# Half of the modulation blocks computed on ScalarE and GpSimd instead of TensorE, in a two-layer diffusion backbone on one core

## The chip, the cores and the metric

The kernel runs on one core of one Trainium2 chip. A core has five engines, each with its own queue that it works off in order: PE (TensorE: matmuls, and transposes done as matmuls), DVE (VectorE), ACT (ScalarE), POOL (GpSimd) and SP, which here only issues DMAs. PE writes to PSUM (banks of 128 rows x 512 f32), everything else lies in SBUF. The metric is device time in microseconds (us), the median of three runs. A change of under 0.2% (some 3 us) can't be told from none.

## What is computed

Two layers over 256 latent and 256 context tokens of width 1024. A conditioning vector per sample (`c`) and one for the context (`c_ctx`) give, by a product with `w_mod`, six vectors of 1024 per layer: shift, scale and gate of the token mixer, and of the feed-forward part.

```python
for l in range(2):
    mod  = silu(c)     @ w_mod[l] + b_mod[l]     # 6 x 1024, for the latent tokens
    modc = silu(c_ctx) @ w_mod[l] + b_mod[l]     # 6 x 1024, for the context tokens
    sh1, sc1, gt1, sh2, sc2, gt2 = split(mod, 6)
    h  = rms_norm(xl, g_pre_mix[l]) * (1 + sc1) + sh1
    y  = token_mixer(h, ...)      # conv, attention and pooling branch, gated, projected
    xl = xl + gt1 * rms_norm(y, g_post_mix[l])
    h  = rms_norm(xl, g_pre_ffn[l]) * (1 + sc2) + sh2
    xl = xl + gt2 * rms_norm(swiglu(h, ...), g_post_ffn[l])
    # context tokens: the same with modc, in layer 0 only
```

The conv branch is a gated product, a depthwise convolution of 31 taps over 512 channels, a layer norm, SiLU and a projection. The attention branch has 8 heads of differential attention; each head's output is normalised (sub-norm).

## The kernel before

Activations lie with channels on the 128 partitions and tokens along the free axis: 512 tokens in layer 0, and in layer 1, where the context is needed for keys and values alone, 256 for most products. Each f32 operand is split into two f32r parts, hi and lo; a product is three matmuls (`mm3`, lines 331 to 333: hi·hi, hi·lo, lo·hi). Weights come in 302 units of 128x1024 f32, in the order of `weight_order`. For each unit SP loads `raw`, ACT writes `hi` (L347), DVE writes `lo = raw - hi` (L348); there are four buffers of each, so a unit is made ready some four units ahead of its matmuls.

A modulation block (`mod_block`) is 256 of the 6144 columns of `w_mod`, for both vectors: 24 blocks a layer, numbered `4*j + part`, where j is 0 to 5 for sh1, sc1, gt1, sh2, sc2, gt2. `mod_product` does eight f32 matmuls (L380; the trace has two records for each) of 32 columns, four of which stand side by side in the array. `mod_close` then brings the sums into place: for shifts and scales ACT copies them out, PE transposes them twice (L422), DVE reduces them into `modv`; for the gates (j of 2 and 5) ACT and DVE split them, PE spreads them over 128 rows by two matmuls a vector (L400, L401), DVE adds the bias and multiplies with the norm's gain into `G`. Blocks stand between other PE work: at the start, within the heads, within the last gating round (`new_modv_fill`), in the feed-forward, and under the end of each output projection.

Layer 0 runs: heads; the conv branch's gated product (`glu`); four pooling groups (`pool_group`: POOL sums of 256 to 271 columns); sub-norm; then three gating rounds of eight steps, `merge(1, ..)`, `merge(2, ..)`, `merge(0, ..)`, each step two units (24 matmuls of 512 columns for the gate, 24 or 12 for the branch). After each step of the first round ten convolution taps are queued on DVE (`S_B`), after each of the second twenty (`S_C`), until all 120 (L832) are out; then `norm`: POOL sums the four accumulators (L839, L842), PE takes the mean (L845), DVE subtracts it (L852), squares, a second matmul (L862), and so to `ya`, which `merge(0, ..)` reads. Then the output projection and the feed-forward follow. The queues' orders are fixed when the program is built, by a scheduler that plays the program through with its own costs.

Of the kernel before, what the change touches and what calls it, by code (L numbers as in the profile page):

```python
# [48 lines left out]
UW = 1024  # L50

# [144 lines left out]
def lay_mod(w):  # L196

    m = w["w_mod"].reshape(DEPTH, 2, 4, P, 24, 256)
    return np.ascontiguousarray(m.transpose(0, 4, 1, 3, 2, 5)).reshape(
        DEPTH * 48, P, UW)  # L200


class Net:
    def __init__(self, ctx, tc, io):
# [15 lines left out]
    BUFS = {"raw": 4, "hi": 4, "lo": 4, "rawx": 4, "hix": 2, "lox": 3, "mod": 2, "H": 4, "V": 18, "O": 8, "Q": 10,  # L220
            "E": 7, "A": 6, "T": 4, "S": 2, "G": 4, "row": 2, "rows": 3, "sq": 4, "K2": 2, "QD": 1, "QH": 2, "QL": 2, "tp": 2, "st": 25, "sh": 1,
# [130 lines left out]
    def mod_load(self, l, b, tag=None):  # L352

        raws = []
        src = self.io["wmod"]
        for kh in range(2):
            if tag is None or len(tag[0]) > 1:
                raw = self.t("mod" if tag is None else tag.popleft(), [P, UW])
                self.nc.sync.dma_start(out=raw, in_=src[l * 48 + b * 2 + kh])
# [27 lines left out]
    def mod_close(self, l, b, ps, gate=None):  # L387
# [155 lines left out]
    def out_proj(self, l, kind, nkp, acts, ntt, x, jg, tail, last, fill=()):  # L543
# [32 lines left out]
        for hf, kp in seq[:-last]:  # L576
            work(hf, kp, self.unit(kind, l, hf, kp), range(ntt))
            self.step(1)
        us = [(hf, kp, self.unit(kind, l, hf, kp)) for hf, kp in seq[-last:]]
# [168 lines left out]
    def subln(self, os, sg, n):  # L748

        nc = self.nc  # L750
        nh = len(os)
        ssq = self.ps(self.SUB_BK)
# [12 lines left out]
        for h in range(nh):  # L765
            bc = self.ps(self.BC_BK)
            rp = slice(32 * h, 32 * h + 32)
            pick = self.ident_r[rp, h:h + 1].to_broadcast([32, P])
            nc.tensor.matmul(bc[:, :n], pick, rh[rp, :n], start=True, stop=False)
            nc.tensor.matmul(bc[:, :n], pick, rl[rp, :n], start=False, stop=True)  # L770
# [7 lines left out]
    def glu(self, l, acts, n, after_first):  # L778
# [3 lines left out]
        for i in range(NCC):  # L782
# [9 lines left out]
            if i == 0 and after_first is not None:  # L792
                after_first()
# [3 lines left out]
    def conv_tasks(self, l, us, nseq, out):  # L797
# [20 lines left out]
        def tap(i, d):  # L818
            def f():
# [5 lines left out]
                if i in by_pool:  # L825
                    t = self.c2("tp")[:, 0:b - a]
# [104 lines left out]
    def layer(self, l, H, acts, first, xin, xnext, tail):  # L931
# [12 lines left out]
        if not need_ctx:  # L944
            us = self.glu(l, acts, n, None)
# [7 lines left out]
        self.new_G(l, 2)  # L953
        fill = deque(range(8, 12))
# [20 lines left out]
        if need_ctx:  # L975
            us = self.glu(l, acts, n, None)
# [45 lines left out]
        for n_ in range(KC):  # L1022
            merge(1, n_, yb, ("ao", l, n_), 0)
            self.step(self.S_B)
# [15 lines left out]
        for n_ in range(KC):  # L1040
            merge(2, n_, yc, ("po", l, n_ // 2) if n_ % 2 == 0 else None,
                  (n_ % 2) * 4)
            self.step(self.S_C)
        self.drain()
        x = self.load_x(xin, ntt, "Q")
        self.new_modv_fill(l)
        for n_ in range(KC):
            merge(0, n_, ya, ("co", l, n_ // 2) if n_ % 2 == 0 else None,
                  (n_ % 2) * 4)
            if self.fill:  # L1050
                self.fill.popleft()()
            if n_ >= 4 and self.fill:
                self.fill.popleft()()
        while self.fill:
            self.fill.popleft()()
# [23 lines left out]
        if need_ctx:  # L1079
            self.new_G(l, 5)  # L1080
        fill = todo
# [24 lines left out]
        for i in range(i0, NFF):  # L1106
# [5 lines left out]
            if fill:  # L1112
                self.mod_block(*fill.popleft(), bank=self.FF_BK)
        while fill:
# [3 lines left out]
        if need_ctx:  # L1118
            ahead = [((l + 1, 12), None), ((l + 1, 16), "OOOO"), ((l + 1, 13), "OOOO")]
        self.out_proj(l, "fo", NFF // 2, fa, ntt, x, 5, tail, self.LASTF[l],  # L1120
                      ahead)

    def new_modv_fill(self, l):

        self.fill = deque()
        for part in range(4):
            for j in (3, 4):
                if l > 0 and (part, j) in ((0, 3), (0, 4), (1, 3)):
                    continue
                self.fill.append(lambda b=j * 4 + part: self.mod_block(l, b, bank=self.FL_BK))  # L1130
# [11 lines left out]
    def run(self):  # L1142
        nc, io = self.nc, self.io
        self.prm, self.modv, self.G = {}, {}, {}
        self.perm = self.sb.tile([P, NPERM], F32, tag="perm", name="perm", bufs=1)
# [12 lines left out]
        perm_r = self.sb.tile([P, 6], F32R, tag="permr", name="perm_r", bufs=1)  # L1158
# [4 lines left out]
        self.eps = self.perm[:, M_EPS:M_EPS + 1]  # L1163
        nc.vector.memset(self.eps, EPS)
# [17 lines left out]
        H, acts = self.new_H()  # L1182
        for tt in range(4):
            junk = (self.c2("T"), self.c2("T"))
            r = self.stats(x[tt], junk)
            for i in range(2):
                nc.vector.tensor_scalar(x[tt][i], x[tt][i], r, None, op0=ALU.mult)

# [8 lines left out]
        def first(kp):  # L1197
            for j in (1, 0):
                self.mod_block(0, 4 * j + kp, loads[kp, j], "s")
            for c in (2 * kp, 2 * kp + 1):  # L1200
                pt = self.ps("t")
                i, cs = c // 4, slice((c % 4) * P, (c % 4 + 1) * P)
                for tt in range(4):
                    nc.tensor.transpose(pt[:, tt * P:(tt + 1) * P], x[tt][i][:, cs],
                                        self.ident)
# [90 lines left out]
```

## Time and profile before

| | |
|---|---|
| median of 3 runs | 1556.02 us (1555.68 to 1558.39) |
| the profiled execution | 1556.86 us, its span 1555.1 us |
| PE, share of the span that it is busy | 98% |
| DVE, ACT, POOL | 63%, 48%, 12% |
| mean granted clock of PE | 0.996 |

A row of busy time can be a union of overlapping records: matmuls are pipelined, so one lasts about 0.39 us in the trace while the next starts after 0.23 us. An arrow `<-DVE rows L348` names what the engine had waited for before the instruction.

### The profile page before, as it was taken

What the parts mean: (1) busy time and instruction counts of PE and PEld (TensorE: products, weight loads), DVE (VectorE), ACT (ScalarE), POOL (GpSimd) and SP (SyncE); (2) the same over time, 40 slices, a digit from 0 to 9 for tenths busy, and PEclk for the clock granted to TensorE, in tenths of its full rate; (3) what the DMA queues carried; (4) which work ended last, traced back from release to release, by engine and by line L of the source; (5) the groups of instructions that cost most, each with busy time, mean ns of one, the idle gap of its engine ahead of it and who ended that gap; (6) DMA issues with size and microseconds to landing.
All of it is one profiled execution on the core that took longest, in us unless ns stands there. A gap on an engine that the chain in (4) does not pass through costs nothing.

```text
span 1555.1 us, 22537 instructions
## 1 busy us (share of the span) xinstructions
PE 1518.8 (98%) x8616; PEld 1253.0 (81%) x8616; DVE 974.6 (63%) x1580; ACT 752.0 (48%) x1284; POOL 192.4 (12%) x216
## 2 busy tenths in 40 slices
PE   6999999999999999999999999998999999999998
PEld 3788878878777688877888888887789799799986
DVE  4588787999964347334333222899998656665554
ACT  5467768532353236322222221865677665554443
POOL 0000100630131100000000000054134212000000
PEclk9999999999999999999999999999999999999999
DMA  9643342232335644446322235534244675556553
GB/s 344 207 121 99 105 133 95 71 123 91 132 116 186 205 141 149 148 169 203 100 95 95 95 118 167 198 106 144 93 137 158 240 254 192 188 177 210 182 189 110
DMA packets 81693, 236.70 MB, mean 152 GB/s; under 512 B 9648, under 2 KB 18480, under 8 KB 81584
## 3 DMA queue, kind: packets, MB, share of 16 engines
q1 hardware_dynamic: 81584, 235.26, 45.7%
q8 instruction: 67, 1.10, 0.3%
q14 instruction: 42, 0.34, 0.1%
HBM read 223.69 MB, written 5.24 MB: 147 GB/s over the span
## 4 chain that ended last, share of the span: by engine, by line
PE 71%; DVE 9%; issue 1%; ACT 1%; DVEq 0%; ACTq 0%
PE psg L332 11%; PE psg L331 11%; PE psg L333 11%; PE pss L331 10%; PE pss L333 10%; PE pss L332 10%; DVE O L832 2%; PE pso L332 2%; PE pso L333 2%; PE pso L331 2%; DVE lo L348 1%; DVE Q L832 1%; PE pss L380 1%; PE pst L380 1%; PE pss L701 1%
## 5 line engine op out<-in xcount | busy, mean ns | idle before, releaser
L347 ACT ACTIVATE hi<-raw 128x1024 fp32r<-128x1024 f32 x299 | 315.2, 1056 | 528.7 <-PE psg L332 162.3
L348 DVE TENSOR_TENSOR lo<-raw,hi 128x1024 fp32r<-128x1024 f32 x299 | 375.5, 1256 | 294.0 <-ACT hi L347 290.0
L331 PE MATMUL psg<-H,hi 128*128 128x512 f32 (+1 forms) x864 | 300.0, 349 | 1.3 <-ACT H L347 0.9
L332 PE MATMUL psg<-H,hi 128*128 128x512 f32 (+1 forms) x864 | 299.4, 347 | 0.7 <-DVE H L348 0.7
L333 PE MATMUL psg<-H,lo 128*128 128x512 f32 (+1 forms) x864 | 299.5, 347 | 0.0
L331 PE MATMUL pss<-H,hi 128*128 128x256 f32 (+1 forms) x704 | 236.7, 337 | 0.1
L332 PE MATMUL pss<-H,hi 128*128 128x256 f32 (+1 forms) x704 | 235.3, 334 | 0.0
L333 PE MATMUL pss<-H,lo 128*128 128x256 f32 (+1 forms) x704 | 234.6, 333 | 0.0
L331 PEld LDWEIGHTS psg<-H,hi 128*128 128x128 f32 x864 | 162.1, 188 | 28.9 <-issue 3.2
L332 PEld LDWEIGHTS psg<-H,hi 128*128 128x128 f32 x864 | 162.4, 188 | 25.1 <-issue 3.8
L333 PEld LDWEIGHTS psg<-H,lo 128*128 128x128 f32 x864 | 162.4, 188 | 22.1 <-issue 1.8
L331 PEld LDWEIGHTS pss<-H,hi 128*128 128x128 f32 x704 | 132.2, 188 | 17.1 <-issue 2.5
L333 PEld LDWEIGHTS pss<-H,lo 128*128 128x128 f32 x704 | 133.8, 190 | 14.9
L332 PEld LDWEIGHTS pss<-H,hi 128*128 128x128 f32 x704 | 133.0, 189 | 14.0
L832 DVE SCALAR_TENSOR_TENSOR Q<-Q,perm,Q 128x482 f32<-128x482 f32 (+14 forms) x120 | 99.4, 828 | 2.5
L829 POOL TENSOR_TENSOR O<-O,tp 128x241 f32<-128x241 f32 (+14 forms) x30 | 24.6, 820 | 473.6 <-ACT tp L827 471.5
L707 ACT ACTIVATE E<-pss,st 128x512 f32<-128x512 f32 (+1 forms) x96 | 58.7, 613 | 38.1 <-DVE st L704 33.0
L1087 DVE TENSOR_TENSOR S<-pss,S 128x256 f32<-128x256 f32 (+1 forms) x43 | 23.8, 554 | 80.8 <-PE pss L333 80.8
L331 PE MATMUL psg<-V,hi 128*128 128x512 f32 (+1 forms) x192 | 64.5, 341 | 3.3 <-ACT S L1003 3.1
L1015 POOL TENSOR_TENSOR O<-O,S 128x512 f32<-128x512 f32 (+1 forms) x32 | 43.9, 1373 | 188.2 <-DVE S L1013 169.4
L332 PE MATMUL psg<-V,hi 128*128 128x512 f32 (+1 forms) x192 | 65.0, 339 | 0.8 <-DVE V L348 0.8
L333 PE MATMUL psg<-V,lo 128*128 128x512 f32 (+1 forms) x192 | 64.5, 337 | 0.0
(373 smaller groups left out, 2638.5 us busy)
## 6 DMA issues: line engine op xcount, KB each, us to landing
raw<-w SPq DMA_DIRECT2D x297, 512.0 KB, 3.4
mod<-wmod SPq DMA_DIRECT2D x66, 512.0 KB, 4.6
A<-wmod SPq DMA_DIRECT2D x18, 256.0 KB, 5.4
O<-wmod SPq DMA_DIRECT2D x16, 256.0 KB, 4.9
QD<-T SPq DMA_DIRECT2D x32, 128.0 KB, 2.4
E<-wmod SPq DMA_DIRECT2D x14, 256.0 KB, 5.3
row<-b_mod SPq DMA_DIRECT2D x24, 128.0 KB, 4.0
xs<-Q SPq DMA_DIRECT2D x12, 256.0 KB, 2.1
```

Source lines behind the costliest of these rows:

```text
L331: mm(out, sh, mh, start=start, stop=False)
L332: mm(out, sh, ml, start=False, stop=False)
L333: return mm(out, sl, mh, start=False, stop=stop)
L347: return (self.nc.scalar.activation(hi, src, AF.Copy), (lo_eng or self.nc.vector).tensor_tensor(out=lo, in0=src, in1=hi.bitcast(F32), op=A ...
L348: (lo_eng or self.nc.vector).tensor_tensor(out=lo, in0=src, in1=hi.bitcast(F32), op=ALU.subtract))
L380: ins = nc.tensor.matmul(ps[32 * kk:32 * kk + 32, 0:256], self.cc[:, k, :], raws[k], start=(k < 4), stop=(k >= 4), tile_position=(0, 32 * ...
L701: nc.tensor.matmul(pss[j][:, :n], q[a][:, j, qt * P:(qt + 1) * P], k[:, j, k0:NT], start=(a == 0), stop=(a == 1))
L707: nc.scalar.activation(e[:, :n], pss[j][:, :n], AF.Exp, bias=mx[:, j:j + 1], accum_out=ss[:, j:j + 1])
L829: nc.gpsimd.tensor_tensor(out=accs[i][:, a:b], in0=accs[i][:, a:b], in1=t, op=ALU.add)
L832: last[0] = nc.vector.scalar_tensor_tensor(out=av, in0=uv, scalar=prm[:, w:w + 1], in1=av, op0=ALU.mult, op1=ALU.add)
L1015: nc.gpsimd.tensor_tensor(out=m[:, :n], in0=m[:, :n], in1=gs[:, :n], op=ALU.add)
L1087: nc.vector.tensor_tensor(out=s[:, :n], in0=pg[:, :n], in1=s[:, :n], op=ALU.mult)
```

## The change

Twelve blocks of each layer are taken from PE. They are named in `WIDE`, as pairs (512 columns): in layer 0 all of j = 3, 4 and 5, in layer 1 the second halves of j = 0, 1, 3 and 4 and all of j = 2. For each, the columns' weights lie so that every partition holds eight rows of 512; ACT multiplies a row by the partition's entry of the vector, POOL adds it to an accumulator, and at the end PE sums over the partitions with a matmul of ones. With two vectors a pair has 16 ACT products, 14 POOL sums, 2 ACT and 2 POOL instructions for hi and lo, and 4 matmuls; with one vector half of that. There are twelve pairs and, in all, 20 accumulators (sixteen of the eight pairs with two vectors, four of the others): 160 ACT products, 140 POOL sums, 20 more on each for hi and lo, 40 matmuls. A pair is cut into four parts that are called out of the program's loops (`wide(1)`); its closing stands after the first part of the next pair. Layer 0's first four pairs stand in `glu` (one), the first gating round (two) and the first half of the second (one); the other eight in layer 0's feed-forward and its projection. Layer 1's heads keep one block (17) in place of four, `new_modv_fill` goes.

Besides, the normalised input is transposed token tile by token tile into SBUF (`XT`) instead of chunk by chunk where it is used; the heads' scales are spread by a weight over all 128 rows instead of 32; `V` has 16 buffers instead of 18; some blocks' loads go into other tiles.

```diff
+WIDE = ((6, 7, 8, 9, 10, 11), (1, 3, 4, 5, 7, 9))
...
-    BUFS = {"raw": 4, "hi": 4, "lo": 4, "rawx": 4, "hix": 2, "lox": 3, "mod": 2, "H": 4, "V": 18, "O": 8, "Q": 10,
-            "E": 7, "A": 6, "T": 4, "S": 2, "G": 4, "row": 2, "rows": 3, "sq": 4, "K2": 2, "QD": 1, "QH": 2, "QL": 2, "tp": 2, "st": 25, "sh": 1,
+    BUFS = {"raw": 4, "hi": 4, "lo": 4, "rawx": 4, "hix": 2, "lox": 3, "mod": 2, "mr": 2, "mt": 2, "ma": 2, "H": 4, "V": 16, "O": 8, "Q": 10,
+            "E": 7, "A": 6, "T": 4, "S": 2, "G": 4, "row": 2, "rows": 3, "sq": 4, "K2": 2, "QD": 1, "QH": 2, "QL": 2, "XT": 2, "st": 25, "sh": 1,
...
+    def wide_tasks(self, l, b):
+        nv = 2 if l < DEPTH - 1 or b < 4 else 1
...
+                for kk in range(2):
+                    k = 2 * q + kk
+                    src = self.c2("mr")
+                    dma = nc.sync.dma_start(out=src, in_=self.io["wmod"][
+                        l * 48 + 4 * b + q, :, kk * 512:(kk + 1) * 512])
+                    self.after(self.last_dma, dma)
+                    for v in range(nv):
+                        t = self.c2("mt" if k else "ma")
+                        nc.scalar.activation(t, src, AF.Copy, scale=self.cc[:, k, v:v + 1])
+                        if k == 0:
+                            accs[v] = t
+                        else:
+                            nc.gpsimd.tensor_tensor(out=accs[v], in0=accs[v], in1=t,
+                                                    op=ALU.add)
+                self.wide_late()
+                if q == 3:
...
+                        self.split(*hl[v], acc, nc.gpsimd)
+                    self.late = lambda: self.wide_close(l, b, hl)
...
+    def wide_close(self, l, b, hl):
+        for v, (hi, lo) in hl.items():
+            ps = self.ps("t")
+            one = self.one_r.to_broadcast([P, P])
+            nc.tensor.matmul(ps, one, hi, start=True, stop=False)
+            nc.tensor.matmul(ps, one, lo, start=False, stop=True)
+            if j in (2, 5):
...
+            nc.vector.tensor_tensor(out=pv, in0=pv,
+                                    in1=self.ident.unsqueeze(1).to_broadcast([P, 4, P]),
+                                    op=ALU.mult)
+            nc.vector.tensor_reduce(out=d, in_=pv, axis=AX.X, op=ALU.add)
...
-            rp = slice(32 * h, 32 * h + 32)
-            pick = self.ident_r[rp, h:h + 1].to_broadcast([32, P])
+            pick = self.ident_r[:, h:h + 1].to_broadcast([P, P])
...
-        fill = deque(range(8, 12))
+        fill = deque(range(8, 12)) if need_ctx else deque([17])
...
         for n_ in range(KC):
             merge(1, n_, yb, ("ao", l, n_), 0)
+            self.wide(1)
             self.step(self.S_B)
...
             self.step(self.S_C)
+            self.wide(1)
...
-        self.new_modv_fill(l)
...
+            for k in [(l, b) for b in WIDE[l][4:]] + [(l + 1, b) for b in WIDE[l + 1]]:
+                self.wq.extend(self.wide_tasks(*k))
...
+            if i >= 4:
+                self.wide(1)
```

Two places show what the queues hold now. The first is POOL, from the last sum of layer 0's pooling groups (`A`) on. Before, what follows are the convolution's sums (`row`) and the additions of the second gating round (`O`):

```order
L924 TENSOR_TENSOR A_3076<-A_3076,V_3090 128x256
L839 TENSOR_TENSOR row_4017<-Q_3225,Q_3455 128x512
L842 TENSOR_TENSOR row_4017<-row_4017,Q_3685 128x512
L1015 TENSOR_TENSOR O_3223<-O_3223,S_3866 128x512
L1015 TENSOR_TENSOR O_3300<-O_3300,S_3935 128x512
```

Now the same end of the pooling groups is followed by pair 7's sums (`ma` the accumulators of the two vectors, `mt` the products from ACT), its lo parts (`sq`), and pair 8:

```order
L1022 TENSOR_TENSOR A_3158<-A_3158,V_3172 128x256
L473 TENSOR_TENSOR ma_3321<-ma_3321,mt_3504 128x512
L473 TENSOR_TENSOR ma_3323<-ma_3323,mt_3507 128x512
L473 TENSOR_TENSOR ma_3321<-ma_3321,mt_3512 128x512
L473 TENSOR_TENSOR ma_3323<-ma_3323,mt_3515 128x512
L473 TENSOR_TENSOR ma_3321<-ma_3321,mt_3596 128x512
L473 TENSOR_TENSOR ma_3323<-ma_3323,mt_3599 128x512
L473 TENSOR_TENSOR ma_3321<-ma_3321,mt_3604 128x512
L473 TENSOR_TENSOR ma_3323<-ma_3323,mt_3607 128x512
L358 TENSOR_TENSOR sq_3611<-ma_3321,sq_3610 128x512
L358 TENSOR_TENSOR sq_3615<-ma_3323,sq_3614 128x512
L473 TENSOR_TENSOR ma_3697<-ma_3697,mt_3703 128x512
```

Between the end of the pooling groups and the last sum of the convolution's accumulators POOL now has 42 instructions of pairs 7, 8 and 9 that it had not (10, 16 and 16); six more of pair 7 stand among the pooling groups' own.

The second place is PE, where the mean of the convolution's accumulators is taken (`pso<-row`). Before, it stands within the gate's unit of step 4 of the second round (`psg<-H`), 18 of its 24 matmuls done:

```order
L331 MATMUL psg_4112<-H_99,hi_3850 128x512
L332 MATMUL psg_4112<-H_101,hi_3850 128x512
L333 MATMUL psg_4112<-H_99,lo_3851 128x512
L845 MATMUL pso_4021<-row_4017,perm 128x512
L331 MATMUL psg_4112<-H_99,hi_3850 128x512
L332 MATMUL psg_4112<-H_101,hi_3850 128x512
```

Now it stands within the branch's product of step 5 (`psg<-V`), and that step's gate and one more branch product come first:

```order
L342 MATMUL psg_4511<-V_4039,hi_4169 128x512
L343 MATMUL psg_4511<-V_4038,lo_4170 128x512
L341 MATMUL psg_4511<-V_4048,hi_4169 128x512
L342 MATMUL psg_4511<-V_4049,hi_4169 128x512
L943 MATMUL pso_4311<-row_4307,perm 128x512
L343 MATMUL psg_4511<-V_4048,lo_4170 128x512
```

The mean has moved back by 50 of the layer's own matmuls (6 + 12 + 24 + 8); by then the four pairs' closings, 16 matmuls, have been done, and one `mod_product` is gone.

## Rows read from the trace of the kernel before

**Rows 1.** The page: the span, and each engine's busy time, share of the span and instructions.

```profile
span 1555.1 us, 22537 instructions
PE 1518.8 (98%) x8616; PEld 1253.0 (81%) x8616; DVE 974.6 (63%) x1580; ACT 752.0 (48%) x1284; POOL 192.4 (12%) x216
```

**Rows 2.** Busy time of each engine by stretch. The stretches are: a part of the start; heads and `glu` of layer 0; from its first convolution tap to its last (end of `glu`, pooling groups, sub-norm, first gating round and half of the second); most of the feed-forward of layer 0; the first heads of layer 1; the time of one low clock.

```profile
core 0: us, PE busy (x) PEld busy (x) DVE busy (x) ACT busy (x) POOL busy (x), PEclk, DMA share, GB/s
20.00:40.00 20.00, 19.41 (x124) 10.38 (x124) 9.37 (x23) 9.20 (x17) 0.00 (x0) 1.00 1.03 366
208.00:279.20 71.20, 71.15 (x383) 56.92 (x382) 51.34 (x106) 51.63 (x98) 0.88 (x5) 1.00 0.35 115
279.20:433.40 154.20, 153.11 (x685) 120.94 (x684) 150.69 (x182) 53.02 (x73) 50.08 (x61) 1.00 0.31 104
600.00:850.00 250.00, 249.66 (x1259) 199.72 (x1260) 96.50 (x146) 78.12 (x116) 0.00 (x0) 1.00 0.40 133
1040.00:1120.00 80.00, 72.71 (x383) 58.28 (x382) 79.68 (x155) 45.56 (x91) 26.08 (x25) 0.98 0.35 113
1113.94:1117.35 3.41, 3.41 (x10) 2.65 (x9) 3.41 (x10) 2.62 (x5) 0.00 (x0) 0.50 0.00 0
```

**Rows 3.** PE in order of time (start us, duration us) around blocks: first two matmuls that spread two heads' scales by a weight over 32 rows (left out behind them are two gate matmuls, at 315.84 and 316.17); then two transposes and a product of blocks in the third gating round; last a gate block with two vectors in the feed-forward. One matmul behind each block (at 492.46, 497.08, 701.56) is left out, and the gate block's own.

```profile
315.09 0.39 PE L331 MATMUL psg<-H,hi 128*128 128x512 f32 x1
315.41 0.50 PE L769 MATMUL pst<-row,perm_r 32*128 32x512 f32 x2
...
316.41 0.39 PE L331 MATMUL psg<-H,hi 128*128 128x512 f32 x1
...
492.09 0.39 PE L333 MATMUL psg<-H,lo 128*128 128x512 f32 x1
492.32 0.38 PE L422 MATMUL pss<-perm,rows 128*128 128x128 f32 x2
...
492.78 0.40 PE L332 MATMUL psg<-H,hi 128*128 128x512 f32 x1
...
495.53 0.39 PE L332 MATMUL psg<-Q,hi 128*128 128x512 f32 x1
495.76 0.39 PE L333 MATMUL psg<-E,lo 128*128 128x512 f32 x1
496.08 1.07 PE L380 MATMUL pss<-mod,perm 128*32 128x256 f32 x16
...
497.42 0.39 PE L332 MATMUL psg<-H,hi 128*128 128x512 f32 x1
...
699.26 0.40 PE L333 MATMUL pss<-H,lo 128*128 128x512 f32 x1
...
701.90 0.40 PE L332 MATMUL pss<-H,hi 128*128 128x512 f32 x1
```

**Rows 4.** What PE waited for: us in total, times, longest.

```profile
PE pst L1204 <- DVE V L1187: 9.9, 2, 8.8
PE pst L400 <- DVE rows L348: 4.2, 2, 2.3
```

**Rows 5.** DVE in the stretch of the taps, by line: busy us, mean ns of one.

```profile
L832 DVE SCALAR_TENSOR_TENSOR Q<-Q,perm,Q 128x482 f32<-128x482 f32 (+14 forms) x120 | 99.4, 828 | 2.5
L348 DVE TENSOR_TENSOR lo<-raw,hi 128x1024 fp32r<-128x1024 f32 (+1 forms) x26 | 32.8, 1260 | 0.4 <-ACT hi L347 0.4
L1013 DVE TENSOR_TENSOR S<-psg,S 128x512 f32<-128x512 f32 x3 | 2.1, 685 | 0.5 <-PE psg L333 0.5
```

**Rows 6.** In order of time: a tap with POOL idle, then three POOL sums of 512 columns, and the tap that each met.

```profile
429.59 0.73 DVE L832 SCALAR_TENSOR_TENSOR Q<-Q,perm,Q 128x490 f32<-128x490 f32 x1
...
395.00 1.46 POOL L842 TENSOR_TENSOR row<-row,Q 128x512 f32<-128x512 f32 x1 [30.46 <-DVE Q L832]
412.81 1.73 POOL L1015 TENSOR_TENSOR O<-O,S 128x512 f32<-128x512 f32 x1 [16.36 <-DVE S L1013]
427.31 1.71 POOL L1015 TENSOR_TENSOR O<-O,S 128x512 f32<-128x512 f32 x1 [5.33 <-DVE S L1013]
...
395.35 1.63 DVE L832 SCALAR_TENSOR_TENSOR Q<-Q,perm,Q 128x482 f32<-128x482 f32 x1
413.42 1.66 DVE L832 SCALAR_TENSOR_TENSOR Q<-Q,perm,Q 128x508 f32<-128x508 f32 x1
427.91 1.65 DVE L832 SCALAR_TENSOR_TENSOR Q<-Q,perm,Q 128x492 f32<-128x492 f32 x1
```

**Rows 7.** The last sum of the accumulators on POOL, and the mean on PE, in order of time.

```profile
433.51 2.15 POOL L842 TENSOR_TENSOR row<-row,Q 128x512 f32<-128x512 f32 x1 [4.48 <-DVE Q L832]
...
438.29 1.02 PE L845 MATMUL pso<-row,perm 128*128 128x512 f32 x2
```

**Rows 8.** By line and shape, the whole span: a reduction of 512 columns out of PSUM on DVE, and a product of 512 columns from SBUF on ACT.

```profile
L704 DVE TENSOR_REDUCE st<-pss 128x1 f32<-128x512 f32 x64 | 42.5, 676 | 5.6 <-PE pss L701 5.4
L755 ACT ACTIVATE sq<-O 128x512 f32<-128x512 f32 x8 | 5.1, 632 | 0.1
```

**Rows 9.** The clock's fall in layer 1's heads, in order of time: the wait before it and the matmuls on either side.

```profile
1113.14 0.38 PE L400 MATMUL pst<-rows,perm_r 128*128 128x256 f32 x1 [1.84 <-DVE rows L348]
...
1114.58 0.63 PE L331 MATMUL pso<-hi,H 128*128 128x512 f32 x1
1115.01 0.63 PE L332 MATMUL pso<-lo,H 128*128 128x512 f32 x1
```

More of the change, by code (lines that the diff above doesn't have):

```diff
@@ L198, in lay_mod @@
     m = w["w_mod"].reshape(DEPTH, 2, 4, P, 24, 256)
-    return np.ascontiguousarray(m.transpose(0, 4, 1, 3, 2, 5)).reshape(
-        DEPTH * 48, P, UW)
+    m = np.ascontiguousarray(m.transpose(0, 4, 1, 3, 2, 5)).reshape(DEPTH * 48, P, UW)
+    for l in range(DEPTH):
+        for b in WIDE[l]:
+            q = w["w_mod"][l][:, b * 512:b * 512 + 512].reshape(4, 2, P, 512)
+            m[l * 48 + 4 * b:l * 48 + 4 * b + 4] = q.transpose(0, 2, 1, 3).reshape(4, P, UW)
+    return m
 class Net:
@@ L437, in mod_close, with part, f @@
                                            op0=ALU.add, op1=ALU.mult)
+    def wide_tasks(self, l, b):
+        nc = self.nc
+        nv = 2 if l < DEPTH - 1 or b < 4 else 1
+        accs = {}
+        def part(q):
+            def f():
+                for kk in range(2):
[3 more added lines that the diff above has]
+                        l * 48 + 4 * b + q, :, kk * 512:(kk + 1) * 512])
+                    self.after(self.last_dma, dma)
+                    for v in range(nv):
[8 more added lines that the diff above has]
+                if q == 3:
+                    hl = {}
+                    for v, acc in accs.items():
+                        hl[v] = self.c2("sq", F32R), self.c2("sq", F32R)
+                        self.split(*hl[v], acc, nc.gpsimd)
+                    self.late = lambda: self.wide_close(l, b, hl)
+            return f
+        return [part(q) for q in range(4)]
@@ L439, in new_modv, with wide, wide_late @@
+    def wide(self, n):
+        while n > 0 and self.wq:
+            self.wq.popleft()()
+            n -= 1
+        if not self.wq and n > 0:
+            self.wide_late()
+    def wide_late(self):
+        late, self.late = self.late, None
+        if late is not None:
+            late()
     def new_modv(self, l):
@@ L751, in subln @@
         nh = len(os)
+        self.wide_late()
         ssq = self.ps(self.SUB_BK)
@@ L776, in subln, with glu @@
         return acts
-    def glu(self, l, acts, n, after_first):
+    def glu(self, l, acts, n):
         nc = self.nc
@@ L975, in layer @@
         if need_ctx:
-            us = self.glu(l, acts, n, None)
+            self.wq.extend(t for b in WIDE[l][:4] for t in self.wide_tasks(l, b))
+            us = self.glu(l, acts, n)
             taps, norm = self.conv_tasks(l, us, nseq, ya)
@@ L1118, in layer @@
         if need_ctx:
-            ahead = [((l + 1, 12), None), ((l + 1, 16), "OOOO"), ((l + 1, 13), "OOOO")]
+            ahead = [((l + 1, 12), ["K2", "QD"]), ((l + 1, 16), "OOOO"), ((l + 1, 13), "OOOO")]
         self.out_proj(l, "fo", NFF // 2, fa, ntt, x, 5, tail, self.LASTF[l],
                       ahead)
[L1123 to L1130, printed above, removed]
     def load_x(self, src, ntt, tag):
@@ L1182, in run @@
         H, acts = self.new_H()
+        xt = [self.t("XT", [P, 4, NT]) for _ in range(2)]
         for tt in range(4):
@@ L1187, in run @@
                 nc.vector.tensor_scalar(x[tt][i], x[tt][i], r, None, op0=ALU.mult)
+            for i in range(2):
+                pt = self.ps("t")
+                for c in range(4):
+                    nc.tensor.transpose(pt[:, c * P:(c + 1) * P],
+                                        x[tt][i][:, c * P:(c + 1) * P], self.ident)
+                nc.scalar.activation(xt[i][:, :, tt * P:(tt + 1) * P],
+                                     pt.rearrange("p (c t) -> p c t", c=4), AF.Copy)
         for kp in range(4):
@@ L1200, in first @@
             for c in (2 * kp, 2 * kp + 1):
[L1201 to L1205, printed above, removed]
+                pt = xt[c // 4][:, c % 4, :]
                 h = self.c2("T")
```

60 lines of the change are left out of this document (42 added, 18 removed).

## The prediction, made before the changed kernel was run

> **What bounds the kernel now.** I read the page's first part, then busy time by stretch, then PE's waits, then PE and DVE in order of time. The page shows PE busy for 1518.8 of 1555.1 us [rows 1]. So nearly every microsecond of PE work that goes is a microsecond won, as long as no other engine becomes late. Busy time by stretch shows where one could: in layer 0, from the first convolution tap to the last, DVE is busy for 150.69 of 154.2 us and POOL for 50.08; in the feed-forward of layer 0 DVE has 96.5 of 250, ACT 78.12 and POOL nothing; in layer 1's heads DVE has 79.68 of 80 [rows 2]. The kernel is thus bound by PE, with a stretch of 154 us in which DVE is just as full. The change takes work from PE everywhere, and puts part of it on POOL and DVE in that stretch.
>
> **PE's share of the change.** In steady work a matmul of 512 columns starts 0.23 us after the last (495.53 to 495.76) [rows 3]. With that I price a block by the stretch it opens up between neighbours. Product: from 495.76 to 497.42 there are 1.66 us, two matmuls would take 0.46, so 1.20. Two transposes: 492.09 to 492.78 is 0.69, less 0.46, so 0.23. A block of shifts or scales costs 1.4 us. A gate block with two vectors: 699.26 to 701.90, 2.64 less 0.46, so 2.2. One with a single vector has no row; it lies between the two, and I take 1.7. What goes is 16 x 1.4 + 4 x 2.2 + 4 x 1.7 = 38 us. What comes is 40 closing matmuls of 512 columns, 40 x 0.23 = 9.3 us. Net, PE loses 28.7 us of work.
>
> Smaller gains. In layer 1's heads, PE waits 4.2 us at L400 for DVE, in gate blocks that go [rows 4]; after one such wait of 1.84 us the records show the clock at 0.50, its lower level of 1.2 GHz, for 3.4 us, matmuls 0.43 us apart [rows 9, 2]. DVE stays full there, so I count 4 us of these some 6. Two scale matmuls with a weight over 32 rows: 315.09 to 316.41 holds five matmuls in 1.32 us where five take 1.16, so 0.16 for a pair; 16 heads in two layers, hi and lo, are 16 such pairs, 2.5 us, the half of them with 256 columns perhaps less: 2 us. At the start PE waits 8.8 us for the normalised input [rows 4]; transposing each token tile as it comes fills some of that, but the DMA engines are at 1.03 then [rows 2], so the weights may be late next: between 0 and 3, I take 2. Sum of the gains: 28.7 + 4 + 2 + 2 = 36.7 us.
>
> In the feed-forward and the projection of layer 0 stand eight of the twelve pairs. ACT gets 16 products of 0.632 us a pair [rows 8], some 10 us; four to five pairs in its stretch of 250 us make it 78 + 50, POOL's sums find POOL empty, and DVE has 150 us free to be held up in. The closing is queued two units behind ACT's and POOL's last work on it. I cost that at nothing; if the cover failed at one closing, PE would wait for one chain of a product and a sum, about 3 us.
>
> **What is added in the full stretch.** Four pairs stand there or just ahead. Two terms are counted in rows: eight closings ahead of the last tap, each a multiplication out of PSUM (0.685, as L1013 [rows 5]) and a reduction (0.676 [rows 8]), 8 x 1.36 = 11 us. The order puts three more `lo` (1.260) and three more L1013 ahead of the last tap: 5.9 us [rows 5].
>
> The third is the price of 48 POOL sums of 512 columns beside taps. The trace shows what a single one does: a tap takes 0.73 us with POOL idle and 1.63, 1.66 and 1.65 when it meets such a sum, 0.92 more [rows 6]. By that the upper bound is 48 x 0.92 = 44. The lower: over all taps the mean is 0.828 against 0.73, 120 x 0.098 = 11.8 us for POOL's 50.08 [rows 5, 2]; a sum alone has no row, and at 1.46 us at most [rows 6] 48 of them would cost 70 x 0.235 = 16. I take 39: the three single meetings are the nearest rows, and taps and `lo`, which read two operands in SBUF, are 132 of DVE's 150.69 us [rows 5, 2], so 88% of 44. Two more L1015 sums now meet taps as well: 2 x 0.92 = 1.8. In all DVE gets 11 + 5.9 + 39 + 1.8 = 58 us before its last tap, and had 3.5 free.
>
> The Trainium skill bears on this (SBUF — State Buffer, Who interferes with whom): DVE and GpSimd share a port pair under an exclusive lock, and whichever comes second is held for the whole of the other's instruction. The three meetings agree in kind, and their 0.92 is less than the 1.46 to 1.73 that the POOL rows last. By the rule at its full length 48 sums would cost at least 70 us, not 39; that is a rival below.
>
> What PE can do meanwhile: it used to reach the mean at 438.29, when the last sum had ended at 433.51 + 2.15 = 435.66 [rows 7], so 2.6 us were to spare. The mean now stands 50 matmuls later (11.6 us) and behind 16 closing matmuls (3.7), and a product less (1.2): 14.1. So PE waits for 58 - 16.7 = 41 us, as branch products and gates have all been put ahead and weights come through the same DVE queue; a part may show as waits on `lo`, but it is one delay.
>
> Two more. After the mean comes the chain to `ya`, and 50 matmuls less stand between it and `merge(0, ..)`; this may cost 0 to 11.6, I take 4, since the order keeps three steps between. Pair 6 in `glu` puts 10 us of ACT's work into a stretch where ACT and DVE are busy 51.6 and 51.3 of 71.2 [rows 2]: 0 to 10, I take 2.
>
> **Sum.** -36.7 + 41 + 4 + 2 = +10 us. On the profiled execution of 1556.9 that is 1567; the median of the runs is 0.8 lower, so I forecast **1566 us**. By its own bounds (sums at 30 to 44, `ya` and pair 6 at their ends) 1556 to 1578.
>
> **Rivals.**
> 1. *The sums slip in.* POOL's sums cost what its work has cost on average, 16 instead of 39. The pooling groups speak for it: POOL is busy 50 us there for 12 us of longer taps. Against it: those are mostly sums of half the columns, and DVE has no free time. PE then waits 41 - 23 = 18: 1566 - 23 = **1543**, faster. Should the taps' end not be waited for at all, 1566 - 41 = 1525.
> 2. *The chain ACT, POOL, ACT.* ACT works in order, and `mt` has two buffers: from the third product on ACT waits for POOL's sums. These are queued behind the pooling groups, whose last sum of `A` comes first, and behind ACT's products stands its share of the sub-norm, on which `merge(1, ..)` depends. It decides from the point where the first product is queued before POOL is done with pooling. Price: some five sums held by as many taps, 5 x (1.7 + 0.7) = 12 us, and after a wait of that kind a low clock [rows 9]. 1566 + 14 = **1580**, slower.
> 3. *Longer locks.* At 1.46 us a sum, 70 instead of 39: 1566 + 31 = **1597**, slower. It is what the skill's rule (SBUF — State Buffer, Who interferes with whom) would give at its word; the taps of 1.65 speak against it.
> 4. *The blocks filled time that was free.* Then taking them out brings less than it measures: where PE waits anyway, in layer 1's heads most of all (DVE 79.68 of 80 [rows 2]), the four blocks' time comes back as other waits. With 12 us less gain: **1578**, slower. PE's 98% speaks against it.
>
> **How the numbers follow.** A difference under 0.2%, 3 us, can't be told from none here. Forecast 0.42 (0.36 slower, 0.06 the same). The first rival 0.33 (0.29 faster, 0.04 the same), no wait at all 0.05, faster. The second 0.11, the third 0.04, the fourth 0.05, all slower. So faster 0.34, the same 0.10, slower 0.56. The range goes from below the first rival, 1534, to 1588, above the second and the fourth: outside stay the case without any wait, the longer locks, and a little of the first rival.
>
> **What would show it.** PE's busy time should fall by some 29 us; the L400 waits should be gone. In the stretch of the taps POOL's busy time should double, and the taps' mean rise to 1.1 us, DVE staying above 95%. PE should show waits of some 40 us in layer 0's first and second gating rounds, on DVE's `lo` or at the mean (now L943) on POOL's `row`. Feed-forward stretches should hold no new wait at the closings. The forecast is wrong if taps stay near 0.85 us (first rival), if ACT waits for POOL and the first gating round for the sub-norm (second), or if PE's busy time falls by less than 20 us (fourth).

## The result, and the profile after

| | before | after |
|---|---|---|
| median of 4 runs | 1556.28 us | 1578.94 us |
| ratio of the times | | 1.0145 (95%: 1.0128 to 1.0163) |
| span of the profiled execution | 1555.1 us | 1576.1 us |

The change makes the kernel 22.7 us slower. The forecast was 10 us slower, 1566 us, with a range up to 1588.

The page of the changed kernel, against [rows 1]:

```profile
span 1576.1 us, 22311 instructions
PE 1504.8 (95%) x8216; PEld 1255.6 (80%) x8216; DVE 1046.8 (66%) x1571; ACT 860.0 (55%) x1450; POOL 441.6 (28%) x376
```

PE has 400 records less, and its busy time fell by 14 us, where the work taken away was worth 29. Most of the rest is time that PE worked at its lower clock: the mean granted clock is 0.983 instead of 0.996, and the second experiment below, with the same 8216 records and a clock of 0.994, has PE busy for 1492.1 us, 26.7 less than before. And PE is idle for 71.3 us instead of 36.3.

Busy time by stretch, for the stretches of [rows 2] as they lie now (the second is heads and `glu` of layer 0, the third goes from the first tap to the last, the fourth is the feed-forward, the fifth the first heads of layer 1):

```profile
core 0: us, PE busy (x) PEld busy (x) DVE busy (x) ACT busy (x) POOL busy (x), PEclk, DMA share, GB/s
20.00:40.00 20.00, 18.38 (x114) 10.03 (x113) 10.47 (x24) 9.67 (x18) 0.00 (x0) 1.00 1.05 388
208.00:284.10 76.10, 72.40 (x391) 58.34 (x390) 56.68 (x105) 61.70 (x114) 23.93 (x25) 1.00 0.38 121
284.10:493.40 209.30, 181.62 (x734) 139.13 (x733) 204.37 (x209) 89.24 (x133) 132.87 (x107) 0.93 0.31 107
640.00:890.00 250.00, 248.81 (x1166) 204.22 (x1165) 121.08 (x145) 126.05 (x191) 100.89 (x67) 1.00 0.43 144
1074.00:1154.00 80.00, 72.49 (x373) 58.59 (x372) 79.73 (x154) 45.67 (x93) 28.06 (x26) 0.98 0.29 99
```

The stretch of the taps lasts 209.3 us, before 154.2. DVE is busy for 204.37 of them; it was full before and is full now, and it has 54 us more to do. PE, full before, is busy for 181.62, and its clock is 0.93. In the feed-forward POOL works 100.89 of 250 us and PE is still busy for 248.81.

DVE by line in that stretch, against [rows 5], then POOL:

```profile
L930 DVE SCALAR_TENSOR_TENSOR Q<-Q,perm,Q 128x482 f32<-128x482 f32 (+14 forms) x120 | 128.9, 1075 | 2.2
L358 DVE TENSOR_TENSOR lo<-raw,hi 128x1024 fp32r<-128x1024 f32 (+1 forms) x28 | 42.0, 1500 | 2.4 <-ACT hi L357 2.4
L507 DVE TENSOR_TENSOR pst<-pst,perm 128x512 f32<-128x512 f32 x8 | 5.3, 690 | 0.0
L511 DVE TENSOR_REDUCE perm<-pst 128x4 f32<-128x512 f32 x6 | 3.8, 680 | 0.0
```

```profile
L473 POOL TENSOR_TENSOR ma<-ma,mt 128x512 f32<-128x512 f32 x42 | 69.2, 1673 | 43.1 <-ACT mt L469 42.4 <-ACT ma L469 0.7
```

The taps, unchanged in number, take 1.075 us in the mean and not 0.828, the `lo` 1.500 and not 1.260. L507 and L511 are the closings.

Where the time goes along the program is read by counting: both kernels have the same 7200 matmuls in `mm3`, and I compare when the k-th of them starts in either trace.

| k, place | before | after | after less before |
|---|---|---|---|
| 0, first | 23.42 | 21.30 | -2.1 |
| 900, last pair of `glu` | 278.69 | 281.23 | +2.5 |
| 1260, behind the sub-norm | 366.19 | 382.66 | +16.5 |
| 1680, behind the mean | 466.51 | 511.55 | +45.0 |
| 1740, third gating round | 480.67 | 533.15 | +52.5 |
| 2040, output projection | 561.61 | 602.73 | +41.1 |
| 3960, end of layer 0's feed-forward | 1004.80 | 1039.39 | +34.6 |
| 5040, third round of layer 1 | 1235.81 | 1257.82 | +22.0 |
| 7140, end | 1535.11 | 1556.36 | +21.2 |

From the start to the third gating round PE loses 54.6 us; from there on it wins back 31.2. What PE waited for, of the same trace (us in total, times, longest):

```profile
PE pst L1287 <- DVE V L1283: 8.8, 1, 8.8
PE psg L341 <- ACT S L1103: 8.4, 1, 8.4
PE pst L493 <- POOL sq L358: 7.8, 2, 5.7
PE psg L341 <- ACT E L357: 5.4, 1, 5.4
PE psg L341 <- DVE O L1108: 4.7, 2, 3.8
PE pst L392 <- DMA mod<-wmod: 2.6, 2, 1.6
```

The waits at L400 of [rows 4] are gone. At the mean itself (L943) PE hardly waits. It waits earlier: at the closing of pair 8, where ACT's `sq` waits for POOL's sums and keeps the sigmoid behind it (8.4), and at the closing of pair 9, directly for POOL (7.8). Later it waits for `ya` (5.4). PE around the closing of pair 9 and at the mean, and POOL in the same time:

```profile
476.01 0.49 PE L492 MATMUL pst<-sq,perm_r 128*128 128x512 f32 x1 [1.11 <-ACT sq L357]
478.69 0.80 PE L493 MATMUL pst<-sq,perm_r 128*128 128x512 f32 x1 [2.19 <-POOL sq L358]
485.58 0.80 PE L493 MATMUL pst<-sq,perm_r 128*128 128x512 f32 x1 [5.66 <-POOL sq L358]
...
494.58 0.40 PE L342 MATMUL psg<-V,hi 128*128 128x512 f32 x1
494.81 1.10 PE L943 MATMUL pso<-row,perm 128*128 128x512 f32 x2
```

```profile
481.64 1.68 POOL L1115 TENSOR_TENSOR O<-O,S 128x512 f32<-128x512 f32 x1 [3.00 <-DVE S L1113]
483.29 2.24 POOL L358 TENSOR_TENSOR sq<-ma,sq 128x512 fp32r<-128x512 f32 x1
491.56 1.29 POOL L1115 TENSOR_TENSOR O<-O,S 128x512 f32<-128x512 f32 x1 [6.03 <-DVE S L1113]
493.45 1.29 POOL L940 TENSOR_TENSOR row<-row,Q 128x512 f32<-128x512 f32 x1 [0.60 <-DVE Q L930]
```

Both closings have something of DVE ahead of them. The last `lo` part of pair 9 on POOL (483.29) stands behind an addition that waited 3.00 us for DVE's `S`. At pair 8's closing ACT had been idle for 9.04 us before, for the pair's weights (`mr`); SP issued them at 410.61, right behind loads of `raw`, and between 400 and 412 SP waited for DVE's `lo`. ACT's first product after that, and SP's waits (total, times, longest):

```profile
414.64 1.33 ACT L469 ACTIVATE mt<-mr,perm 128x512 f32<-128x512 f32 x2 [9.04 <-DMA mr<-wmod]
SPq L305 <- DVE lo L358: 11.0, 2, 7.0
```

So two readings are open. Either DVE decides (the last accumulator sum ends at 494.74, the mean starts at 494.81), and the waits before it are only the form in which its delay shows. Or the waits of ACT and PE for POOL's sums are the loss, and the mean happened to be reached just then.

### The profile page after: what moved, and what is told of

It reads as the page before. It is cut to its first block, busy times and chain, and to the rows that moved or that the text cites. A ratio compares the mean times of both kernels' runs of the same rounds, so it can differ in the third digit from the quotient of the medians.

```text
span 1576.1 us, 22311 instructions
## 1 busy us (share of the span) xinstructions
PE 1504.8 (95%) x8216; PEld 1255.6 (80%) x8216; DVE 1046.8 (66%) x1571; ACT 860.0 (55%) x1450; POOL 441.6 (28%) x376
## 4 chain that ended last, share of the span: by engine, by line
PE 78%; DVE 13%; issue 3%; ACT 3%; DMA 2%; POOL 1%; SPq 0%; DVEq 0%; ACTq 0%; POOLq 0%
PE psg L341 12%; PE psg L343 12%; PE psg L342 12%; PE pss L342 9%; PE pss L343 9%; PE pss L341 9%; DVE Q L930 4%; PE pso L343 3%; PE pso L341 3%; PE pso L342 3%; DVE lo L358 3%; PE pss L800 2%; DMA mr<-wmod 2%; DVE O L930 1%; PE pst L831 1%
## 5 line engine op out<-in xcount | busy, mean ns | idle before, releaser
L358 DVE TENSOR_TENSOR lo<-raw,hi 128x1024 fp32r<-128x1024 f32 x299 | 388.1, 1300 | 248.0 <-ACT hi L357 241.7
L473 POOL TENSOR_TENSOR ma<-ma,mt 128x512 f32<-128x512 f32 x140 | 212.1, 1535 | 313.7 <-ACT mt L469 311.5
L341 PEld LDWEIGHTS psg<-H,hi 128*128 128x128 f32 x864 | 164.5, 191 | 34.8 <-DVE O L1108 4.3
L342 PEld LDWEIGHTS psg<-H,hi 128*128 128x128 f32 x864 | 164.5, 190 | 22.9 <-DVE H L358 1.3
L341 PEld LDWEIGHTS pss<-H,hi 128*128 128x128 f32 x704 | 133.6, 190 | 18.5 <-ACT H L357 3.0
L469 ACT ACTIVATE mt<-mr,perm 128x512 f32<-128x512 f32 x140 | 94.4, 714 | 68.4 <-DMA mr<-wmod 67.8
L930 DVE SCALAR_TENSOR_TENSOR Q<-Q,perm,Q 128x482 f32<-128x482 f32 (+14 forms) x120 | 128.9, 1075 | 2.2
L710 POOL TENSOR_TENSOR sh<-sh,perm 128x256 f32<-128x256 f32 x32 | 30.4, 949 | 253.4 <-DVE sh L707 187.5
L341 PE MATMUL psg<-V,hi 128*128 128x512 f32 (+1 forms) x192 | 65.6, 350 | 3.3 <-ACT V L357 2.1
```

What stands on the lines that cost most here:

```text
L341: mm(out, sh, mh, start=start, stop=False)
L342: mm(out, sh, ml, start=False, stop=False)
L358: (lo_eng or self.nc.vector).tensor_tensor(out=lo, in0=src, in1=hi.bitcast(F32), op=ALU.subtract))
L469: nc.scalar.activation(t, src, AF.Copy, scale=self.cc[:, k, v:v + 1])
L473: nc.gpsimd.tensor_tensor(out=accs[v], in0=accs[v], in1=t, op=ALU.add)
L710: nc.gpsimd.tensor_tensor(out=sh, in0=sh, in1=self.sin, op=ALU.mult)
```

## The experiments

**1. The pairs of the stretch back on PE.** Pairs 6 to 9 leave `WIDE`; their eight blocks stand in the third round.

```diff
-WIDE = ((6, 7, 8, 9, 10, 11), (1, 3, 4, 5, 7, 9))
+WIDE = ((10, 11), (1, 3, 4, 5, 7, 9))
...
+            if back:
+                self.mod_block(l, back.popleft(), bank=self.FL_BK)
...
```

> Pairs 6 to 9 of layer 0 are computed on PE again, as eight blocks in the third gating round; the other eight pairs stay on ACT and POOL. Theory (the whole loss lies in the stretch of layer 0's taps, where the four pairs' work delays DVE): the start and everything behind the third round keep what the changed kernel shows there, -2 and -20 us against the kernel before, so about 1534 us. Rival (part of the loss is the pairs' in the feed-forward, or the other edits'): 1545 us or more.

Measured: 1535.25 us, 0.986 of before (0.9844 to 0.9877). The four pairs bring the whole loss; the eight others and the smaller edits together win 1.4%.

**2. Short sums.** `accs[v][:, :8]` in pairs 6 to 9; POOL's `lo` parts keep their 512 columns.

```diff
-    nc.gpsimd.tensor_tensor(out=accs[v], in0=accs[v], in1=t, op=ALU.add)
+    w = 8 if l == 0 and b < 10 else 512
+    nc.gpsimd.tensor_tensor(out=accs[v][:, :w], in0=accs[v][:, :w], in1=t[:, :w], op=ALU.add)
```

> In pairs 6 to 9 of layer 0 POOL adds only 8 of the 512 columns, so shifts and scales of the second half of layer 0 lack most of their sum; number and order of the instructions and their waits stay. Theory (contention: each of these sums costs DVE some 0.8 to 0.9 us): the last tap ends 40 to 45 us earlier than in the changed kernel, taps' mean back from 1.08 to about 0.83 us, and the time falls to about 1535 to 1542 us. Rival (DVE's own added work, closings and lo, counts, contention does not): the time falls by under 12 us.

Measured: 1539.97 us. DVE and POOL by line in the stretch:

```profile
L931 DVE SCALAR_TENSOR_TENSOR Q<-Q,perm,Q 128x482 f32<-128x482 f32 (+14 forms) x120 | 102.6, 855 | 2.2
L358 DVE TENSOR_TENSOR lo<-raw,hi 128x1024 fp32r<-128x1024 f32 (+1 forms) x28 | 34.4, 1233 | 9.1 <-ACT hi L357 9.1
```

```profile
L474 POOL TENSOR_TENSOR ma<-ma,mt 128x8 f32<-128x8 f32 x42 | 20.4, 494 | 65.7 <-ACT mt L469 65.3
```

As many sums of 0.494 us leave the taps at 0.855 us and the `lo` at 1.233. Against the changed kernel that is 26 us less on the taps and 8 on the `lo`, 34 for 42 sums: 0.8 each. The last tap ends 31 us earlier, 9 to 14 less than expected; DVE is now idle for 12.7 us of the stretch, in the changed kernel for 4.9. The time is that of the theory.

**3. Sums that nothing waits for.** The sums stay, in size and place, and read a constant; ACT's products go nowhere; the closing takes an operand from the weights.

```diff
-    nc.gpsimd.tensor_tensor(out=accs[v], in0=accs[v], in1=t, op=ALU.add)
+    add = nc.gpsimd.tensor_tensor(out=accs[v], in0=accs[v] if k > 1 else c, in1=c, op=ALU.add)
...
-    self.split(*hl[v], acc, nc.gpsimd)
+    nc.scalar.activation(hl[v][0], last[v], AF.Copy)
...
+    hl[v] = hl[v][0], hl[v][0]
```

> In pairs 6 to 9 of layer 0 POOL's sums keep number, size and place in POOL's queue but read a constant, ACT's products go nowhere, the closing takes its operand from the weights: so ACT never waits for POOL and PE never for POOL's part of a closing, and shifts and scales of the second half of layer 0 are not computed. Theory (DVE's delay decides, it is one delay whatever waits show it): the waits at the closings vanish, PE waits at the mean instead, which comes within 5 us of where it is, and the time is 1570 to 1579 us. Rival (the chain ACT, POOL, ACT makes the loss): the time falls by 15 us or more, under 1564 us.

Measured: 1582.19 us, 1.0159 of before (1.0144 to 1.0174). PE, and the POOL sum that it waits for:

```profile
490.88 0.40 PE L343 MATMUL psg<-V,lo 128*128 128x512 f32 x1
495.64 2.07 PE L962 MATMUL pso<-row,perm 128*128 128x512 f32 x2 [4.36 <-POOL row L959]
```

```profile
494.32 1.26 POOL L959 TENSOR_TENSOR row<-row,Q 128x512 f32<-128x512 f32 x1 [0.60 <-DVE Q L949]
```

Nothing is won. The sums still hold DVE up: the taps take 1.015 us in the mean. PE waits for `lo` (8.1 us in all) and at the mean, which comes at 495.64, 0.8 us from where it was. The chain of ACT, POOL and ACT isn't the loss here; the second reading falls. The time is 3 us above the range that the theory gave.

**4 and 5. The pairs elsewhere.** Experiment 4 puts pairs 6 and 7 into layer 0's heads and 8 and 9 into its third round, one part a head and a step; experiment 5 adds short sums in 6 and 7.

```diff
+            self.wq.extend(t for b in WIDE[l][:2] for t in self.wide_tasks(l, b))
...
+            self.wide(1)
...
```

> All pairs as in the changed kernel, but those of layer 0 stand elsewhere: 6 and 7 in its heads, 8 and 9 in its third gating round, none in the stretch of the taps. Theory (the place makes the loss): that stretch is as long as before the change, pair 6's and 7's cost in the heads is some 5 us, the rest keeps its gain of 31: about 1528 us. Rival (the chain of ACT and POOL costs PE wherever it stands): new PE waits in heads and third round, 1540 us or more.

> As the experiment that moved layer 0's pairs, but POOL adds only 8 of 512 columns in pairs 6 and 7, which stand in the heads (half of sh2 and sc2 of layer 0 lacks most of its sum). There the heads took 20 us more than with those pairs on PE. First theory (POOL's sums hold DVE up in the heads too): most of it goes, 12 us or more, about 1530 us. Second (ACT's products and the wait of ACT for POOL delay the heads' softmax, and the length of the sums counts little): under 6 us go, 1538 us or more.

Measured: 1543.59 us and 1536.54 us. The first meets the rival's number, not the theory's 1528; the second lies between its two expectations. Counted as above, PE has lost 18.5 us to experiment 1 when `glu` ends (k = 900), and with short sums 11.9: some 7 us come from the sums' length, the larger part from something else that the pairs bring into the heads, ACT's products or its waits. Which, I did not separate; so for the heads the rival isn't excluded.

**6. Two pairs.** 6 and 7 stay in their places, 8 and 9 are four blocks on PE.

```diff
-WIDE = ((6, 7, 8, 9, 10, 11), (1, 3, 4, 5, 7, 9))
+WIDE = ((6, 7, 10, 11), (1, 3, 4, 5, 7, 9))
...
```

> Pairs 6 and 7 stay where the changed kernel has them, pairs 8 and 9 are four blocks on PE in the third round. Theory (DVE's delay counts only beyond what PE has to spare at the mean): a pair and two closings add about 20 us to DVE before its last tap, of which 13 to 16 are covered, so PE's delay in the stretch is some 10 instead of 54 us, and the time is 1538 to 1546 us. Rival (each pair in the stretch costs PE its part): half of the loss stays, about 1555 us.

Measured: 1547.48 us, just above the theory's range. PE's loss, against experiment 1 and counted as above, is 6.7 us when `glu` ends (k = 900) and another 14.4 up to behind the sub-norm (k = 1260), whose output `merge(1, ..)` needs at once. There is nothing to spare there. From there to the third round PE is not idle at all.

**7. The closings' DVE work left out.**

```diff
+            if l == 0:
+                nc.vector.memset(self.modv[l, j][:, 4 * half:4 * half + 4, v], 0.0)
+                continue
```

> The changed kernel with the closings' DVE work of pairs 6 to 9 left out (a small memset in place of multiplication, reduction, bias and gain), so sh2 and sc2 of layer 0 are zero in their second half; PE's closing matmuls and all sums stay. Theory (every microsecond of DVE ahead of the last tap is one of the end): 11 to 13 us less on DVE, the last tap as much earlier, and 1564 to 1569 us. Rival (the closings lie in DVE's gaps, or the waits of ACT and PE for the sums decide): 1574 us or more.

Measured: 1572.74 us, between the two. The last tap ends at 482.6 instead of 493.4, 10.8 us earlier, as the sum had it. But the end came only 6.2 us earlier. PE shows why:

```profile
475.51 0.40 PE L343 MATMUL psg<-H,lo 128*128 128x512 f32 x1
484.90 2.07 PE L946 MATMUL pso<-row,perm 128*128 128x512 f32 x2 [8.99 <-POOL row L943]
```

With other durations the scheduler put the mean elsewhere: 1566 matmuls of `mm3` come before it, in the changed kernel 1616. PE waits 9 us, and has the 50 matmuls (11.6 us) still to do.

**8. Two small edits to experiment 1**, in layer 1: block 17 in the fifth head, and the first block under an output projection in its own tile again.

```diff
-            if h % 2 == 0 and fill:
+            if fill and (h % 2 == 0 if need_ctx else h == 4):
...
-        places = (["K2", "QD"], "AAAA", "AAEE", "EEEE")
+        places = (None, "AAAA", "AAEE", "EEEE")
```

> The kernel with layer 0's four pairs back on PE (1535 us), and two small edits: layer 1's block 17 stands in its fifth head instead of its first, where PE waited 2.2 us for its weights and the clock fell; the first block under an output projection is loaded into its own tile again. If these waits are what is missing there: 1529 to 1533 us. If the waits are taken by others: 1534 to 1537 us.

Measured: 1536.95 us, as expected if others take the waits. The wait for the weights is gone, and in its place PE waits 4.4 us for POOL's `K`.

**9. One pair, behind the sub-norm.** Pair 9 keeps its place; 6 to 8 are six blocks on PE.

```diff
-WIDE = ((6, 7, 8, 9, 10, 11), (1, 3, 4, 5, 7, 9))
+WIDE = ((9, 10, 11), (1, 3, 4, 5, 7, 9))
...
+        if need_ctx:
+            self.wq.extend(self.wide_tasks(l, 9))
...
+        back = deque(range(12, 18)) if need_ctx else deque()
...
```

> Of layer 0's four pairs only pair 9 stays in the stretch, where the changed kernel has it (first half of the second gating round, behind the sub-norm); 6 to 8 are six blocks on PE in the third round. Theory (behind the sub-norm DVE's delay counts only beyond what PE has to spare at the mean, 13 to 16 us; a pair with its two closings adds about that): under 4 us are lost, two blocks and two closings less save 2, so 1531 to 1537 us. Rival (each pair in the stretch costs a quarter of the 54 us): 1545 us or more.

Measured: 1549.56 us. The theory's size fails: 14 us for a single pair. The rival's number is met, but not its rule, as two pairs cost 12 in experiment 6. PE, and the last accumulator sum on POOL:

```profile
442.82 0.49 PE L493 MATMUL pst<-sq,perm_r 128*128 128x512 f32 x1 [2.16 <-POOL sq L358]
451.00 0.79 PE L493 MATMUL pst<-sq,perm_r 128*128 128x512 f32 x1 [7.46 <-POOL sq L358]
453.23 1.22 PE L943 MATMUL pso<-row,perm 128*128 128x512 f32 x1
```

```profile
450.91 2.26 POOL L940 TENSOR_TENSOR row<-row,Q 128x512 f32<-128x512 f32 x1
```

The whole loss, 15.5 us, is at the pair's closing, next to the mean. The sum of accumulators ends at 453.17, and POOL's `lo` part of the pair stands right before it; by the last tap alone, which ends at 449.83, the mean could have come some 2 us earlier, no more. And 1587 matmuls stand before the mean, in experiment 1 it was 1591: here the order put nothing ahead to use the time. What PE has to spare is no fixed 13 to 16 us; it is what the order places there.

**10. Two pairs in the third round**, two parts in each of its first four steps; 6 and 7 on PE.

```diff
+        if need_ctx:
+            self.wq.extend(t for b in (8, 9) for t in self.wide_tasks(l, b))
...
+            self.wide(2)
```

> Pairs 8 and 9 stand in the first four steps of the third round, where DVE has time free, 6 and 7 are four blocks on PE in its second half; nothing stands in the stretch of the taps. If the place decides, four blocks less and eight closing matmuls more save 4 us against all four pairs on PE (1535): 1529 to 1533 us. If ACT's waits for POOL or the last closing hold PE there too, as the moved pairs did at the end of that round (5 us): 1535 us or more.

Measured: 1531.88 us, 0.9829 of before (0.9814 to 0.9844), the fastest of all. Its row for the third round (478 to 555) shows room on DVE and ACT:

```profile
478.00:555.00 77.00, 75.34 (x365) 56.76 (x364) 43.63 (x51) 42.31 (x63) 57.60 (x38) 1.00 0.66 231
```

Put side by side, each from its trace, the runs with pairs in the stretch, and two without:

| kernel | last accumulator sum ends | mean starts | matmuls before it | median us |
|---|---|---|---|---|
| before | 435.65 | 438.29 | 1566 | 1556.3 |
| after | 494.74 | 494.81 | 1616 | 1578.9 |
| 1, none of the four | 438.45 | 440.61 | 1591 | 1535.3 |
| 2, short sums | 464.39 | 464.77 | 1608 | 1540.0 |
| 3, sums unwaited | 495.59 | 495.64 | 1617 | 1582.2 |
| 6, two pairs | 463.07 | 464.59 | 1603 | 1547.5 |
| 7, no closing work | 484.85 | 484.90 | 1566 | 1572.7 |
| 9, one pair | 453.17 | 453.23 | 1587 | 1549.6 |

In each version with such pairs the mean starts 0.05 to 1.5 us after DVE's last tap and POOL's sum allow it. PE's loss up to the mean is about the delay of that sum, less the matmuls that the order put ahead of it. In experiments 2 and 6 this is a match of numbers and not a wait: PE is not idle right before the mean there, and most of its delay came earlier (against experiment 1 it is 16 and 21 us behind at k = 1260). That DVE alone sets the delay at those earlier places is not shown.

## Why the prediction was right or wrong

**What bounds the kernel: right.** A stretch in which DVE is as full as PE was the place of the loss (experiment 1).

**DVE's added work: right in sum.** Forecast were 58 us ahead of the last tap; the 3.5 us of free time named beside them were not taken off, and DVE's idle time did not shrink. The stretch grew from 153.0, measured from its first tap to its last, to 209.3: 56.3. By parts: the sums' contention was forecast at 41 for 50 of POOL's instructions (48 of the pairs, two of L1015). Experiment 2 gives 34 for the 42 that it shortened; at the same 0.8 the other eight would make 6 more, so some 40. The closings were forecast at 11, and cost 10.8 by experiment 7. That leaves some 5 us for the rest, 5.9 in the forecast, DVE's waits for ACT's `hi` (2.4) among them. The rule cited from the Trainium skill (SBUF — State Buffer, Who interferes with whom), by which the second instruction is held for all of the first, agrees in kind: shorter sums hardly cost the taps anything. It also agrees more closely than the prediction made of it. In [rows 6] the three sums end at 396.46, 414.54 and 429.02, and the taps that met them at 396.98, 415.08 and 429.56, each 0.52 to 0.54 us later, where a tap alone takes 0.73. So a tap was held nearly to its sum's end, and it lost less than the sum's length because it began 0.35 to 0.61 us after the sum. In size a sum of 1.673 us cost DVE 0.8, so the third rival, which charged the whole length, fell.

**PE's wait: right in size, wrong in place.** Forecast was 41 us. By the table PE loses 42.5 us from the end of `glu` (+2.5) to behind the mean (+45.0 at k = 1680), of which the closing matmuls, less the product and the scale matmuls there, are about 2: so some 40. The same comes out of DVE's side: 56.3 less 2.6 to spare and 14.1 for the matmuls put ahead is 39.6. Only 27.7 us of it are idle time (1.1 before); part of the rest is PE's work at the lower clock. And it was to show at the mean or at `lo`; it showed at the closings, at the sub-norm and at the sigmoid. Waits named by the profile point to where a delay comes to light, and experiment 3 shows that taking them away only moves it.

**What failed is the size of three terms.** They come to 11 us, the 11 us between +10 and +21 (by the spans).
- Pair 6 in `glu`: 2 forecast; by the table +4.6, from -2.1 to +2.5.
- The chain to `ya`: 4 forecast, +7.5, from 45.0 at k = 1680 to 52.5 at 1740. PE waits 5.45 us there, and then the clock is at its lower level for 6.8 us.
- The gains behind the stretch. Of 36.7 forecast, some 36 lay behind it, once the start, the one block in the stretch, the scale matmuls of layer 0 and the closings in the stretch are set apart; the table shows 31.2. The third round gave 11.4 (9.9 forecast), the closings of the feed-forward cost 0.93 for four matmuls, as priced. Short were the feed-forward and its projection (6.5 where 8.9 were counted), layer 1 up to its third round (12.6 of some 15), and the end (0.8 of some 2). There a block that goes leaves a wait. Before, the last block under layer 1's first output projection stood where PE waited; now it is done earlier, and the wait is there without it; the time from the transposes to the next matmul is 3.4 us, with the block it was 3.7. Before, and after:

```profile
1355.69 0.60 PE L488 MATMUL pst<-perm,S 128*128 128x128 f32 x4
1358.42 1.07 PE L380 MATMUL pst<-mod,perm 128*32 128x256 f32 x16 [2.13 <-ACT T L497]
```

```profile
1375.29 0.60 PE L585 MATMUL pst<-perm,S 128*128 128x128 f32 x4
1378.68 0.80 PE L341 MATMUL pss<-H,hi 128*128 128x256 f32 x2 [2.80 <-ACT H L357]
```

In layer 1's heads the one block that is left waits for its weights (2.6 us by the waits above), and the clock falls for 3.4 us; experiment 8 removed that and found the next wait. This is the fourth rival in the small: some blocks stood in time that was free. How the feed-forward's 2.4 us came to be missing was not traced.

**The rivals.** The first, sums that slip in, falls: taps at 1.075, not 0.85. The second, ACT's chain, is seen in the waits and falls as a cause with experiment 3. It may be part of the cost in the heads of experiment 4. That its 1580 and the fourth's 1578 lie nearest to the measured 1579 is chance: the chain was not the cause, and of the fourth's 12 us less gain under 5 are found. Two of the signs of being wrong came up as well, ACT's waits for POOL and a fall of PE's busy time by 14 us, under 20; the first was only the form of the delay, the second the lower clock.

**The bounds.** The sum of the forecast's own bounds is not 1556 to 1578: with the sums at 30 to 44 and `ya` and pair 6 at their ends it gives 1551 to 1587.

## What to carry to other kernels

Before work is moved to an idle engine, ask what it shares with the engine that is full beside it: POOL was idle two thirds of the stretch, but each of its sums took 0.8 us from DVE. With the same kind of work only where DVE has time to spare (the feed-forward and the third round, experiment 10), the kernel, its smaller edits included, is 26 us faster than before. And read a delay at the point where the late engine's result is needed, not at the waits before it: if the removal of a wait leaves that point where it was, the wait was only where the delay showed.

## What was not expected of the hardware

After the long waits the clock stayed at its lower level (0.50, 1.2 GHz) for longer than the 3.4 us of [rows 9], while PE went on being held up: it is busy for 6.43 of 13.70, 4.34 of 10.20 and 4.16 of 6.80 us. The three such stretches of layer 0 in the changed kernel:

```profile
420.50:434.20 13.70, 6.43 (x14) 4.26 (x15) 13.52 (x15) 7.02 (x11) 5.47 (x4) 0.50 0.20 66
478.50:488.70 10.20, 4.34 (x9) 3.01 (x10) 10.06 (x11) 0.66 (x2) 4.02 (x3) 0.50 0.32 104
522.90:529.70 6.80, 4.16 (x10) 3.29 (x11) 2.92 (x4) 6.74 (x10) 0.00 (x0) 0.50 0.62 188
```

By the account above the first two cost little by themselves, as PE was due to wait for DVE anyway, and the third, behind the last of these waits, is lost; no run separates the clock's part.
